# Operand buffers at multiples of 128 bytes, and score products ordered by their number of rows, in a two-block transformer kernel

## The chip, the cores and the metric

The kernel runs on one core of a Trainium2 chip. The metric is the device time of one launch in microseconds (us), the median of several runs. Engines: PE is TensorE (matrix products; PEld its weight loads), DVE is VectorE, ACT is ScalarE, POOL is GpSimd, SP is SyncE, whose queue here issues nearly all transfers.

## What is computed

256 tokens of width 1024 in float32 go through two transformer blocks of two layers each. The reference, cut to its frame:

```python
def first_block(x, p, ...):                       # 2 layers
    for i in range(2):
        z = rms_norm(h, g_mix[i]) @ w_in[i]
        y_a = chunked_spatial_gating(...)
        y_b = rwkv7_time_mix(...)
        y_c = nsa_attention(...)                  # compressed, selected and window branch; 8 query heads, 2 key groups
        h = h + concat([y_a, y_b, y_c]) @ w_out[i]
        hn = rms_norm(h, g_ffn[i])
        f = swiglu(hn, ...) if i % 2 == 0 else moe_swiglu(hn, router_w, router_b, w1, w3, w2)   # 8 experts, top 2
        h = h + f
        h = h + (p[i] @ ple_proj_w[i]) * sigmoid(rms_norm(h, g_ple[i]) @ ple_gate_w[i])

def second_block(x, ...):                         # 2 layers
    for l in range(2):
        x = x + 0.5 * swiglu(rms_norm(x), gate[l, 0], up[l, 0], down[l, 0])      # width 2816
        proj = rms_norm(x) @ w_in[l]
        ya, yb, yc = neighbourhood(...), diff_attention(...), window_gqa(...)
        g = sigmoid(h @ w_gate[l] + b_gate[l])
        x = x + sum(g_b * (y_b @ w_branch[l, b])) @ w_o[l]
        x = x + 0.5 * swiglu(rms_norm(x), gate[l, 1], up[l, 1], down[l, 1])

def moe_swiglu(x, router_w, router_b, w1, w3, w2):
    logits = x @ router_w + router_b
    top_v, top_i = lax.top_k(logits, 2)           # gate = softmax of the two
    for e in range(8):
        out = out + gate[..., e:e + 1] * swiglu(x, w1[e], w3[e], w2[e])
```

## The kernel before, in words

**The big products.** Weights and activations are split exactly into two float32r parts, high (`wh`) and low (`wl`), and each product is made of three passes (`mm`, L422, the matmul itself is L426): high by high, low by high, high by low. Most have 128 rows, a stationary operand of 128 x 128 (activations: `xT` of a normalised input, `xe` an expert's tokens, `gT` the gated middle of a feed-forward, `yT` an attention's output, `mT` the merged one) and move 512 columns of weights past it; in the profile's rows the moving operand stands first (`ps<-wh,xT`). The rest have the weights as the stationary operand and move 256 tokens (`ps<-xT,wh`).

**The weights.** `Feed` loads 1 MB pieces (`raw`, L193, on SP's queue) as far ahead as it has buffers, in the order of their use. ACT makes the high part (L215) and DVE the low part (L216) of each half. Each phase adds buffers of its own to the three of `wp`: a pool that is opened on top of what the pools below it take, so that a buffer's place depends on the sizes of all tiles ahead of it.

**The scores.** In the second block (`scores`, L1989, called 24 times) one call makes the scores of four heads for 128 queries: two heads `m` of each half `i` of the rows, in a bank for each half. Each is the sum of two products of 256 columns: one over all 128 rows (`ks`, L1996; it opens the sum, start=True) and one over the 64 rows of its half (`kl`, L1997, the remaining low part; it closes the sum, stop=True). They are written head by head, so 128 rows and 64 rows take turns. The first block's `first` in `nsa` (L1247) does the same (L1259, L1260), 16 products of 128 columns a call for the first tile of tokens and 8 of 256 columns for the second. Behind each call DVE takes the maximum (L1361), ACT the exponential (L1363), PE transposes the result (L1370), and products of the gates and branches, or of the RWKV chain, are woven in between.

**The router.** `experts` (L1436) makes the logits and picks two experts per token on DVE (L1485 to L1524); the index of each expert is taken from columns 256 to 263 of `const_moe` (`km["eidx"]`, used at L1493, L1497 and L1509), which is loaded at L1430, ahead of the first expert's weights. Then PE counts (L1515, L1516, L1527), DVE makes one-hot matrices `dp` (L1552), and PE gathers an expert's tokens with them (L1566). Products of the per-layer embedding (`pT`) fill in.

**What sets the order.** Each engine runs its instructions in the order of its queue. The Python code sets that order by generators whose steps are woven by fixed ratios, and a scheduler may move an instruction within it.

Of the kernel before, what the change touches and what calls it, by code (L numbers as in the profile page):

```python
# [22 lines left out]
P = 128  # L23
S = 256
# [11 lines left out]
# Big products run on operands that are split exactly into two float32r parts.  # L36
# [5 lines left out]
AHEAD = 4  # L42
FFN_BUFS = (4, 4)
# [5 lines left out]
# A mix's streams are merged by these numbers of steps: time before the units and its fill; time, units and their fill;  # L49
# the last steps of time and the first half of the output product.  # L50
# [14 lines left out]
def _t5_bucket(rel):  # L65
# [10 lines left out]
    ("gmmask", P), ("reset", 512), ("inv", 8),  # L76
]
_LAYOUTM = [("iota", 2 * P), ("eidx", 8)]
# [17 lines left out]
def _constants():  # L96
# [20 lines left out]
        "gmmask": s <= t, "reset": reset, "inv": np.broadcast_to(inv, (P, 8)),  # L117
# [3 lines left out]
        "eidx": np.broadcast_to(np.arange(8), (P, 8)),  # L121
# [10 lines left out]
    return {"const_ident": np.eye(P, dtype=np.float32), "const_first": c1, "const_moe": cm, "const_counts": np.concatenate([s < t, np.ones((P, P))], 1).astype(np.float32),  # L132
# [3 lines left out]
def _cols(w, at, n, step=512):  # L136
    """Column pieces of w from column at on."""
    return [w[:, c:c + min(step, at + n - c)] for c in range(at, at + n, step)]


def backwards(ap):
    """ap with its last dimension read from the end."""
# [6 lines left out]
class Feed:  # L149
    """The weights in the order of their use, loaded and split into float32r parts ahead of the products."""  # L150
# [12 lines left out]
    def drop(self, phase):  # L163
        """The buffers of a phase go."""
# [4 lines left out]
    def add(self, phase, srcs, split=True, heads=False):  # L169
        """srcs: DRAM [kb*128, n] in the order of their products; heads: columns (g j d) change to (j g d)."""  # L170
# [12 lines left out]
    def load(self):  # L183
        """Starts the next load, if a buffer is free."""
# [41 lines left out]
    def take(self, src):  # L226
        """The next row blocks of src: [(row block, part APs [128, n])]."""
# [6 lines left out]
    def done(self, n=1):  # L234
        """The products with the n oldest row blocks in hand are in the program."""
        for _ in range(n):
            self.free[1].append(self.live.popleft()[1])
# [11 lines left out]
class Operand:  # L249
    """Transposed parts [128, K, 256], put into the program by steps when products are about to need them."""  # L250
# [16 lines left out]
def merge(*streams):  # L267
    """The steps of all, each stream (steps, how many) kept as far along as the others."""
# [16 lines left out]
def weave(main, fill, ratio=1):  # L285
    """The steps of main with ratio steps of fill after each; what is left of fill stays."""
# [1942 lines left out]
```

## Time and profile before

| | |
|---|---|
| median of three runs | 2845.73 us (2842.85 to 2850.19) |
| span of the profiled execution | 2848.1 us; 2.4 us above the median; the page gives no other time for that execution |
| PE busy | 2794.6 us, 98% |
| DVE, ACT, POOL busy | 1911.7, 1652.1, 142.7 us |
| mean granted TensorE clock | 0.976 of full speed |
| moved by DMA | 594 MB, 209 GB/s over the span |

The span runs from the first to the last instruction. By stage: the first block's mixes, its dense feed-forward and embedding gates up to about 680 us, the experts up to about 1490 us, then the second block; its two attentions lie behind 1750 us and 2350 us. A matmul's record begins where the engine takes it up and its end is modelled; consecutive records overlap, so the pace is read from start to start, and the mean duration only shows differences between forms. Windows are given in us from the span's start.

### The profile page before, as it was taken

The page shows a single profiled execution, that of the slowest core. Times are in us where ns is not written, and L with a number is a line of the kernel's source. Part 1 is how long each engine was busy: PE and PEld are TensorE (multiplying, and loading weights), DVE is VectorE, ACT ScalarE, POOL GpSimd, SP SyncE. Part 2 cuts the span into 40 slices and gives each one's busy share as a digit, 9 for nine tenths or more (in the row PEclk, how much of TensorE's full clock was granted, in tenths as well). Part 3 has the DMA queues.
Part 4 walks back from the last instruction along what each step waited for, and adds up shares of the span by engine and source line. Part 5 has one row for each costly group of instructions (what it writes and reads, how often), then busy time and mean ns, then how long its engine had stood idle before and what let it go on. Part 6 is the DMA issues. An engine that isn't in the chain of part 4 may idle for free. (4 is left out here: it accounts for less than half of the span.)

```text
span 2848.1 us, 38806 instructions
## 1 busy us (share of the span) xinstructions
PE 2794.6 (98%) x15206; PEld 2308.7 (81%) x15206; DVE 1911.7 (67%) x2586; ACT 1652.1 (58%) x2277; POOL 142.7 (5%) x183
## 2 busy tenths in 40 slices
PE   8999999999999999999989999999999999999998
PEld 7888887877888888888877888888888888888887
DVE  6446556547989989988886556666555556676554
ACT  6445456436777777777766445664444445664543
POOL 1220001320000000000000000010000000010000
PEclk9889999979999999999999999999999999999999
DMA  6208533307999999999975745444654546444651
GB/s 210 88 21 280 185 127 124 105 16 282 344 338 360 337 347 353 342 348 336 348 247 197 240 156 151 140 137 168 236 185 177 186 137 180 134 141 152 245 191 60
DMA packets 301542, 594.46 MB, mean 209 GB/s; under 512 B 25926, under 2 KB 78886, under 8 KB 301350
## 3 DMA queue, kind: packets, MB, share of 16 engines
q1 hardware_dynamic: 300102, 587.69, 59.8%
q0 software_dynamic: 1248, 4.20, 0.5%
q8 instruction: 122, 2.00, 0.3%
q14 instruction: 70, 0.57, 0.1%
HBM read 590.74 MB, written 1.10 MB: 208 GB/s over the span
## 5 line engine op out<-in xcount | busy, mean ns | idle before, releaser
L216 DVE TENSOR_TENSOR wl<-raw,wh 128x1024 fp32r<-128x1024 f32 (+1 forms) x1098 | 1316.2, 1219 | 605.7 <-ACT wh L215 594.4
L215 ACT ACTIVATE wh<-raw 128x1024 fp32r<-128x1024 f32 x1098 | 1136.8, 1049 | 767.1 <-PE ps L426 715.7
L426 PE MATMUL ps<-wh,xT 128*128 128x512 f32 (+2 forms) x2944 | 919.3, 388 | 11.8 <-ACT xT L419 3.7
L426 PEld LDWEIGHTS ps<-wh,xT 128*128 128x128 f32 x2944 | 544.2, 190 | 133.6 <-DVE xT L420 7.6
L426 PE MATMUL ps<-wl,xT 128*128 128x512 f32 (+2 forms) x1472 | 563.1, 383 | 0.5 <-DVE wl L216 0.5
L426 PE MATMUL ps<-wh,gT 128*128 128x512 f32 x1584 | 504.4, 391 | 0.0
L426 PE MATMUL ps<-wh,xe 128*128 128x512 f32 (+1 forms) x1536 | 458.6, 378 | 0.0
L426 PEld LDWEIGHTS ps<-wh,gT 128*128 128x128 f32 x1584 | 297.2, 188 | 62.0
L426 PEld LDWEIGHTS ps<-wh,xe 128*128 128x128 f32 x1536 | 279.2, 188 | 55.7
L426 PEld LDWEIGHTS ps<-wl,xT 128*128 128x128 f32 x1472 | 279.7, 190 | 53.6 <-DVE wl L216 2.0
L426 PE MATMUL ps<-wl,gT 128*128 128x512 f32 x792 | 309.5, 391 | 0.0
L426 PE MATMUL ps<-wl,xe 128*128 128x512 f32 (+1 forms) x768 | 289.4, 377 | 1.4 <-DVE wl L216 1.2
L426 PE MATMUL ps<-xT,wh 128*128 128x256 f32 x960 | 178.1, 287 | 5.7 <-ACT wh L215 2.9
L426 PEld LDWEIGHTS ps<-wl,gT 128*128 128x128 f32 x792 | 148.8, 188 | 30.9 <-DVE wl L216 0.5
L426 PEld LDWEIGHTS ps<-wl,xe 128*128 128x128 f32 x768 | 144.3, 188 | 32.3 <-DVE wl L216 5.0
L426 PEld LDWEIGHTS ps<-xT,wh 128*128 128x128 f32 x960 | 150.4, 193 | 8.0 <-ACT wh L215 3.1
L426 PE MATMUL ps<-xT,wl 128*128 128x256 f32 x480 | 135.9, 284 | 0.0
L1363 ACT ACTIVATE e<-e,mx 128x256 f32<-128x256 f32 (+1 forms) x160 | 76.1, 477 | 43.9 <-DVE mx L1361 43.5
L426 PEld LDWEIGHTS ps<-xT,wl 128*128 128x128 f32 x480 | 92.2, 193 | 0.3 <-DVE wl L216 0.3
L493 ACT ACTIVATE junk<-x 128x512 bf16<-128x512 f32 x56 | 35.2, 628 | 62.4 <-DVE x L547 47.8
L417 DVE TENSOR_TENSOR gT<-ps,gT 128x512 fp32r<-128x512 f32 (+1 forms) x108 | 66.5, 639 | 6.0 <-ACT gT L416 6.0
L416 ACT ACTIVATE gT<-ps 128x512 fp32r<-128x512 f32 (+1 forms) x108 | 56.9, 551 | 19.2 <-PE ps L485 19.0
(434 smaller groups left out, 2470.2 us busy)
## 6 DMA issues: line engine op xcount, KB each, us to landing
raw<-in_moe_w_dram SPq DMA_DIRECT2D x264, 1024.0 KB, 6.2
raw<-in_w_in_dram SPq DMA_DIRECT2D x50, 1024.0 KB, 5.4
raw<-in_ffn_w_gate_dram SPq DMA_DIRECT2D x44, 1024.0 KB, 5.1
raw<-in_ffn_w_up_dram SPq DMA_DIRECT2D x44, 1024.0 KB, 5.0
raw<-in_ffn_w_down_dram SPq DMA_DIRECT2D x44, 1024.0 KB, 5.5
raw<-in_ffn_w_dram SPq DMA_DIRECT2D x33, 1024.0 KB, 5.1
raw<-in_w_gate_dram SPq DMA_DIRECT2D x24, 1024.0 KB, 5.0
raw<-in_w_branch_dram SPq DMA_DIRECT2D x12, 1024.0 KB, 4.9
```

The source lines that it names most:

```text
L215: nc.scalar.activation(ho, w, AF.Copy)
L216: nc.vector.tensor_tensor(lw, w, ho.bitcast(F32), op=ALU.subtract)
L416: nc.scalar.activation(h, src, AF.Copy)
L417: nc.vector.tensor_tensor(l, src, hf, op=ALU.subtract)
L426: self.nc.tensor.matmul(ps, lhs[p], rhs[q], start=start and i == 0, stop=stop and i == last)
L493: self.nc.scalar.activation(junk, self.x[:, t, h * 512:(h + 1) * 512], AF.Square, accum_out=ss[:, t, h:h + 1])
L1363: nc.scalar.activation(e[:, i], e[:, i], AF.Exp, bias=mx[:, i:i + 1], scale=-1.0, accum_out=sums[:, i:i + 1])
```

## The change

Two parts. **Places of the buffers:** tiles are padded, moved to another pool or share a buffer, so that the buffers of the big products' operands begin at multiples of 128 bytes. In the built programs their places, modulo 128, are:

| phase | weights, before | activations, before | both, after |
|---|---|---|---|
| mixes and dense feed-forward of the first block | 64 | xT 64, gT 64 | 0 |
| experts | 96 | xe 32, gT 96 | 0 |
| second block, first feed-forward | 32 (those of `wp` 64) | xT 64, gT 32 | 0 |
| second block, other three feed-forwards | 96 (`wp` 64) | xT 64, gT 96 | 0 |
| second block, attention and its products | 0 or 64 | xT 64, yT 96, mT 0 | 0 |

For this the expert indices leave `const_moe` and become a tile and a transfer of their own (`eidx`, 128 x 8, 4 KB), issued where the router's steps begin on DVE. **The scores:** `score_products` writes all products of 128 rows of a call first (only the first head of a bank opens it), then all of 64 rows, the halves taking turns (only the last closes it). Engines, shapes and number of products stay as they were; beside the one transfer nothing is added.

```diff
+PERS_REST = 12
-    ("gmmask", P), ("reset", 512), ("inv", 8),
+    ("gmmask", P), ("reset", 512), ("inv", 8), ("rest", 16),
-_LAYOUTM = [("iota", 2 * P), ("eidx", 8)]
+_LAYOUTM = [("iota", 2 * P)]
...
+        self.rb = self.pers.tile([P, NE], F32, name="rb")
...
-        r = self.xp.tile(shape, F32, name=self.nm("rs"), tag=f"rs{shape[1]}", bufs=3)
+        r = self.xp.tile(shape, F32, name=self.nm("rs"), tag=f"rs{shape[1]}", bufs=1 if shape[1] == 8 else 3)
...
-        self.oka = self.pers.tile([P, 4], F32, name="oka")
+        self.oka = self.pers.tile([P, PERS_REST], F32, name="oka")[:, 0:4]
...
-            for i in range(hb):
-                for gg, own, _ in self.halves():
-                    q = qs[t][:, j0 + i, gg]
-                    nc.tensor.matmul(pS[gg][:, i], q, ks[:, br, gg, 0:nk], start=True, stop=False)
-                    nc.tensor.matmul(pS[gg][:, i], q[own], kl[own, br, 0:nk], start=False, stop=True)
+            self.score_products([[(pS[gg][:, i], qs[t][:, j0 + i, gg], ks[:, br, gg, 0:nk], kl[:, br, 0:nk]) for gg in range(2)]
+                                 for i in range(hb)])
...
+        km["eidx"] = T("eidx", [P, NE])
+        nc.sync.dma_start(km["eidx"], a["const_eidx"])
         lg = T("lg", [P, NT, NE])
...
-            mx = T(f"mx{r}", [P, NT])
+            mx = pool.tile([P, NT], F32, name=f"mx{r}", tag=f"mx{r}")
...
-        cnt = T("cnt", [P, 1])
+        cnt = pool.tile([P, NT], F32, name="cnt", tag="mx0")[:, 0:1]
...
-        gs = pool.tile([P, 2], F32, name=self.nm("gs"), tag="gs", bufs=2)
+        gs = pool.tile([P, 16], F32, name=self.nm("gs"), tag="gs", bufs=2)[:, 0:2]
...
+    def score_products(self, heads):
+        last = len(heads) - 1
+        for m, two in enumerate(heads):
+            for ps, q, ks, _ in two:
+                self.nc.tensor.matmul(ps, q, ks, start=m == 0, stop=False)
+        for m, two in enumerate(heads):
+            for (_, own, _), (ps, q, _, kl) in zip(self.halves(), two):
+                self.nc.tensor.matmul(ps, q[own], kl[own], start=False, stop=m == last)
...
-            for m in range(2):
-                for i, own, _ in self.halves():
-                    q = qs[:, m, i, t * P:(t + 1) * P]
-                    nc.tensor.matmul(ps[i][:, m], q, ks[:, kb(m), i], start=True, stop=False)
-                    nc.tensor.matmul(ps[i][:, m], q[own], kl[own, kb(m)], start=False, stop=True)
+            self.score_products([[(ps[i][:, m], qs[:, m, i, t * P:(t + 1) * P], ks[:, kb(m), i], kl[:, kb(m)]) for i in range(2)]
+                                 for m in range(2)])
...
-                    ss = pool.tile([P, 4], F32, name=self.nm("oss"), tag="oss", bufs=2)
+                    ss = pool.tile([P, 4], F32, name=self.nm("oss"), tag="oss", bufs=1)
```

Left out: `tab`, `nsink` and `sink`, padded or moved in the same way, and comments. Lines move by up to three; the score products are L1916 (128 rows) and L1919 (64 rows) in the changed kernel, the big products L428.

**PE, the first score call of the second block** (`ks` are keys of 128 rows, `kl` of 64; `ps_19327` and `ps_19328` are the banks of the two halves). Before:

```order
8240 L426 MATMUL ps_19246<-xT_18858,wl_19175 128x256
8241 L1996 MATMUL ps_19327<-ks_19018,qs_19017 128x256
8242 L1997 MATMUL ps_19327<-kl_19019,qs_19017 128x256
8243 L1996 MATMUL ps_19328<-ks_19018,qs_19017 128x256
8244 L1997 MATMUL ps_19328<-kl_19019,qs_19017 128x256
8245 L1996 MATMUL ps_19327<-ks_19018,qs_19017 128x256
8246 L1997 MATMUL ps_19327<-kl_19019,qs_19017 128x256
8247 L1996 MATMUL ps_19328<-ks_19018,qs_19017 128x256
8248 L1997 MATMUL ps_19328<-kl_19019,qs_19017 128x256
8249 L426 MATMUL ps_19356<-wh_19205,xT_18858 128x512
```

In the changed kernel:

```order
8187 L428 MATMUL ps_19248<-xT_18860,wl_19177 128x256
8188 L1916 MATMUL ps_19329<-ks_19020,qs_19019 128x256
8189 L1916 MATMUL ps_19330<-ks_19020,qs_19019 128x256
8190 L1916 MATMUL ps_19329<-ks_19020,qs_19019 128x256
8191 L1916 MATMUL ps_19330<-ks_19020,qs_19019 128x256
8192 L1919 MATMUL ps_19329<-kl_19021,qs_19019 128x256
8193 L1919 MATMUL ps_19330<-kl_19021,qs_19019 128x256
8194 L1919 MATMUL ps_19329<-kl_19021,qs_19019 128x256
8195 L1919 MATMUL ps_19330<-kl_19021,qs_19019 128x256
8196 L428 MATMUL ps_19358<-wh_19207,xT_18860 128x512
```

Four goes to 64 rows become one. So stand 18 of the 24 calls; in the other six, and in most of the first block's calls, the scheduler puts other products in between or takes the banks one after the other, so that a call has two goes. Over the program there are 152 places before and 46 now where a product of 64 rows follows one of 128 in the score products.

**SP, the first loads of the experts.** Before:

```order
134 L193 DMA raw_5946<-in_moe_w_dram 128x2x1024
135 L193 DMA raw_6200<-in_moe_w_dram 128x2x1024
136 L193 DMA raw_6210<-in_moe_w_dram 128x4x512
137 L193 DMA raw_6233<-in_moe_w_dram 128x4x512
138 L193 DMA raw_6257<-in_moe_w_dram 128x4x512
```

In the changed kernel:

```order
135 L194 DMA raw_5946<-in_moe_w_dram 128x2x1024
136 L1469 DMA eidx<-in_const_eidx_dram 128x8
137 L194 DMA raw_6202<-in_moe_w_dram 128x2x1024
138 L194 DMA raw_6212<-in_moe_w_dram 128x4x512
139 L1543 TENSOR_LOAD cnti
140 L1543 ISA x2
141 L194 DMA raw_6235<-in_moe_w_dram 128x4x512
```

The indices are fetched behind the ninth load of expert weights (`raw_5946`). SP's read of the longest expert list (`cnti`), which stood at the end of the experts, now stands ahead of the twelfth.

**DVE, the router** (`lg` are the logits, `wl` the low part of expert weights). Before:

```order
677 L1490 TENSOR_REDUCE mx_6074<-lg 128x2
678 L1492 TENSOR_TENSOR ne_6076<-lg,mx_6074 128x16
679 L1493 SCALAR_TENSOR_TENSOR ne_6076<-ne_6076,const_moe 128x16
680 L1495 TENSOR_REDUCE first_6079<-ne_6076 128x2
681 L1497 TENSOR_TENSOR oh_6081<-const_moe,first_6079 128x16
```

In the changed kernel:

```order
674 L1491 TENSOR_REDUCE mx_6076<-lg 128x2
675 L1493 TENSOR_TENSOR ne_6078<-lg,mx_6076 128x16
676 L217 TENSOR_TENSOR wl_6205<-raw_5894,wh_6204 128x1024
677 L217 TENSOR_TENSOR wl_6209<-raw_5894,wh_6208 128x1024
678 L1494 SCALAR_TENSOR_TENSOR ne_6078<-ne_6078,eidx 128x16
679 L1510 TENSOR_SCALAR sel<-eidx 128x8
680 L1496 TENSOR_REDUCE first_6081<-ne_6078 128x2
681 L1498 TENSOR_TENSOR oh_6083<-eidx,first_6081 128x16
```

Two splits of weights now stand ahead of the first use of the indices. The second of them waits for PE to be done with the buffer of a late embedding product, and the instruction behind it waits for the transfer of `eidx`. On PE all embedding products now stand ahead of the counts.

## Rows read from the trace of the kernel before

**Rows 1.** The page's first part: busy time and share of the span.
```profile
PE 2794.6 (98%) x15206; PEld 2308.7 (81%) x15206; DVE 1911.7 (67%) x2586; ACT 1652.1 (58%) x2277; POOL 142.7 (5%) x183
```
**Rows 2.** Windows: length, PE, PEld, DVE, ACT, POOL busy, granted clock, DMA.
```profile
700.00:1450.00 750.00, 749.48 (x3626) 617.99 (x3626) 674.47 (x658) 575.85 (x618) 0.00 (x0) 1.00 0.96 346
...
558.20:571.90 13.70, 13.70 (x62) 10.24 (x62) 3.32 (x29) 6.49 (x26) 0.00 (x0) 0.50 0.01 1
...
1493.50:1496.90 3.40, 3.01 (x11) 2.69 (x12) 0.84 (x2) 2.10 (x8) 0.76 (x1) 0.50 0.31 98
```
**Rows 3.** Groups by form on PE, whole span: count, busy, mean ns, idle before.
```profile
L426 PE MATMUL ps<-wl,gT 128*128 128x512 f32 x792 | 309.5, 391 | 0.0
L426 PE MATMUL ps<-wl,xe 128*128 128x512 f32 x640 | 253.8, 397 | 0.9 <-DVE wl L216 0.7
```
**Rows 4.** The same view for 1755 to the end.
```profile
L426 PE MATMUL ps<-wl,xT 128*128 128x512 f32 x720 | 284.9, 396 | 0.0
```
**Rows 5.** Timeline of PE among the experts: start, duration, instruction.
```profile
701.42 0.39 PE L426 MATMUL ps<-wl,xe 128*128 128x512 f32 x1
...
708.42 0.39 PE L426 MATMUL ps<-wl,xe 128*128 128x512 f32 x1
...
710.05 0.62 PE L426 MATMUL ps<-wh,gT 128*128 128x512 f32 x2
...
713.46 0.62 PE L426 MATMUL ps<-wh,gT 128*128 128x512 f32 x2
```
**Rows 6.** Timeline of PE in the second block, a feed-forward's xT products.
```profile
2329.64 0.40 PE L426 MATMUL ps<-wl,xT 128*128 128x512 f32 x1
...
2333.16 0.39 PE L426 MATMUL ps<-wl,xT 128*128 128x512 f32 x1
```
**Rows 7.** Timeline of PE at the first score call of the second block.
```profile
1756.59 0.28 PE L426 MATMUL ps<-xT,wl 128*128 128x256 f32 x1
1756.70 0.28 PE L1996 MATMUL ps<-ks,qs 128*128 128x256 f32 x1
1756.91 0.38 PE L1997 MATMUL ps<-kl,qs 64*128 64x256 f32 x1
...
1759.10 0.50 PE L426 MATMUL ps<-wh,xT 128*128 128x512 f32 x1
```
**Rows 8.** Timeline of PE: products of 64 rows, both halves in turns, elsewhere.
```profile
47.23 0.48 PE L915 MATMUL ps<-tw,waup 64*128 64x256 f32 x1
47.24 0.48 PE L918 MATMUL ps<-zm,waup 64*128 64x256 f32 x1
47.55 0.38 PE L915 MATMUL ps<-tw,waup 64*128 64x256 f32 x1
```
**Rows 9.** Timeline of PE: a score call of 128 columns, first block.
```profile
555.22 0.33 PE L1259 MATMUL ps<-ks,qs 128*128 128x128 f32 x1
...
558.29 0.47 PE L1259 MATMUL ps<-ks,qs 128*128 128x128 f32 x1
```
**Rows 10.** Timeline of ACT and PE behind the second score call.
```profile
1766.25 0.19 ACT L1363 ACTIVATION_READ_ACCUMULATOR e<-e,mx 128x1 f32 x1
...
1767.26 0.93 PE L1370 MATMUL ps<-ident,e 128*128 128x128 f32 x7
```
**Rows 11.** Loads issued at 667.1 and 669.8: counts and starts, time to landing.
```profile
L193 SPq DMA_DIRECT2D raw<-in_moe_w_dram x2: 2582/2583/2584, 667.1 to 669.8; - x2
...
DMA to landing us min/median/max: 14.2/14.2/14.2
```
**Rows 12.** Timeline of DVE and PE: the router's first use of the indices, the first gather.
```profile
676.98 0.18 DVE L1493 SCALAR_TENSOR_TENSOR ne<-ne,const_moe 128x16 f32<-128x16 f32 x1
...
681.50 2.69 PE L1566 MATMUL ps<-dp,xT 128*128 128x128 f32 x20
```
**Rows 13.** Timeline of PE at the end of the experts, with the idle time before.
```profile
1493.89 1.94 PE L525 MATMUL ps<-ident,x 128*128 128x128 f32 x8 [5.45 <-PEq L1543]
```
**Rows 14.** The page's part 5: the low parts of the weights on DVE.
```profile
L216 DVE TENSOR_TENSOR wl<-raw,wh 128x1024 fp32r<-128x1024 f32 (+1 forms) x1098 | 1316.2, 1219 | 605.7 <-ACT wh L215 594.4
```

## Prediction before the run

> **What bounds the kernel now.** The page's first part comes first [rows 1]: PE is busy 98% of the span, DVE 67%, ACT 58%. A busy PE is not yet a PE at its peak, so the windows come next [rows 2]: among the experts PE is busy 749.48 of 750 us and DVE 674.47, which is 90%. The queue of products sets the time there, and time comes out of the span only if the products themselves follow each other faster. So I read PE's timeline from start to start and look for products that take longer than others of the same shape. There are two kinds. The reader should see [rows 5] that thirty products with `xe` start in 708.42 - 701.42 = 7.00 us, 233.3 ns each, and fifteen with `gT` in 713.46 - 710.05 = 3.41 us, 227.3 ns each: same shape, same clock, same engine without a gap. What differs is the place of the buffers (weights 96 and `xe` 32; weights 96 and `gT` 96). And a step between two products of 128 rows takes 0.11 us (1756.59 to 1756.70), the first step to 64 rows 0.21, and the seven steps from 1756.91 to 1759.10, in which rows change every time, 0.313 each [rows 7].
>
> **Places of the buffers.** Nothing is removed or added on PE; the pace of 512-column products is what can change. After the change all places are alike (0 and 0). I take the pace of the alike pair that I have, 227.3 ns.
> - Experts: 640 low-part products [rows 3], each with two high-part ones, so 1920 products; 1920 x (233.3 - 227.3) = 11.5 us. They lie in the stretch where PE has no gap, so this comes off the span if the weights keep up: DVE would then need 674.5 of 738.5 us, 91%.
> - `xT` in the second block from 1755 us on: 3 x 720 = 2160 products [rows 4]. In a plain stretch [rows 6] fifteen take 3.52 us, 234.7 ns each, 7.4 above `gT`; as a mean over all, which holds some pairs that are alike already, the duration is 396 ns against 391 of `gT` [rows 3, 4], 5 above. I take the mean: 2160 x 5 = 10.8 us. The upper end is 2160 x 7.4 = 16.0.
> - First block: places are alike already (64 and 64), so nothing. For the products that move 256 columns no row tells alike from unlike places; I take nothing.
>
> Sum -22 us, with ends -10 (only the experts gain) and -27. The Trainium skill speaks against this term: by the page SBUF — State Buffer, section Who interferes with whom, PE reads the moving operand and the weights through two independent ports that share nothing with each other, so the place of one against the other should not matter and the term would be 0. The rows do not agree with that, with 6 ns per product [rows 5]; but no run here has moved a buffer alone, so this stays as a rival.
>
> **The scores.** A call of the second block now takes 1759.10 - 1756.70 = 2.40 us [rows 7]. Grouped it is made of three steps between products of 128 rows, 3 x 0.11; one step to 64 rows, 0.21; the other half's product, which starts 0.01 later [rows 8]; the step to the second pair; again 0.01; and the step back to 128 rows, 0.31. The step to the second pair is not shown for this shape. It lies between 0.11 (no change of rows) and 0.32 (47.23 to 47.55, the same pattern with other operands [rows 8]); I take 0.22, the middle. Sum 1.09, saving 1.31. For 18 calls 23.6 us. In the six calls that stay in two goes a second pair of changes (0.21 + 0.31) comes back and one pair step goes; they save about 0.9 each, 5.4. Second block: 29 us.
>
> First block: eight calls of 256 columns, mostly in two goes, at 0.9 make 7. The four calls of 128 columns take 0.256 a step (555.22 to 558.29, twelve steps [rows 9]), 4.1 us; grouped, eight steps of at most 0.11, three pair steps of 0.22, changes of 0.52, and for three of them another 0.5: some 2.4. They save 1.7 each, 7. What hides these calls' end is the RWKV chain, in whose small products they are woven; shorter calls can leave PE waiting for it, so I take 11 of these 14. Together -40 us, ends -25 (nothing from the first block, 0.2 less from each call of the second) and -46.
>
> **The expert indices.** The new transfer is small, but it stands in SP's queue behind nine loads of 1 MB. The ninth is issued at 669.8 and lands 14.2 us later, at 684.0 [rows 11]. If transfers of a queue land in order, as these did, the indices are there at about 684.1. DVE wants them at 676.98 [rows 12], so it stands still 7.1 us with the router behind it. From there to the first gather on PE it is 681.50 - 676.98 = 4.52 us, less one split of 1.22 [rows 14] that now lies ahead: gather at 684.1 + 3.3 = 687.4, **5.9 us late**. Before, the embedding products covered the router; they are used up at about 681 whatever happens, so PE then idles. Behind an idle time of 5.45 us at the end of the experts [rows 13] the granted clock was 0.50 (1.2 GHz instead of 2.4) for 3.4 us [rows 2], half a stretch lost, 1.7. I take +7. Lower end +4: were the indices in time, the second split that was moved ahead would still wait for the last embedding products (681) and take 1.22, gather at 685.5. Upper end +12: the loads behind it (the twelfth waits for SP's read of the longest list, which comes from the same chain) arrive late once more. SP's read is then gone from the end of the experts; since the other engines read there as before, I take nothing for it.
>
> The padding, the smaller number of buffers for 1/rms (`rs`, `oss`) and the constant that is 1% longer touch engines with idle time [rows 1]: nothing, and with that cover gone some tenths of a us.
>
> **Sum.** -22 - 40 + 7 = -55 us. Against the profiled span of 2848.1 that is 2793; the span stands 2.4 above the median of the runs, so the forecast for the median is **2791 us**.
>
> **Rivals.**
> - *The softmax becomes the wait.* The last exponential ends at 1766.44 and its transposes begin at 1767.26 [rows 10]: 0.8 us of slack. A call 1.3 shorter brings the transposes 1.3 closer, while DVE may begin only when the bank is closed, now at the call's end rather than half-way, so the softmax moves by about 0.8: 0.3 of slack are left. If one split of weights (1.22) on DVE comes between, 0.9 is lost in each of 24 calls, 22 us: 2813. For it: the slack is small. Against it: splits have been there before, and the fill is long. Chance 0.13.
> - *The places bring nothing*, since something else slows the `xe` and `xT` products: -33, so 2813. Against it: the difference stands in both stretches [rows 5, 6] and goes with the places, not with the stage. Chance 0.10.
> - *The clock gains.* In the first block the clock was at half from 558.20 to 571.90 [rows 2], which begins inside a score call [rows 9]: what PE did before was twelve score products with rows changing. Denser products could keep it up: half of 13.7, 6.9 us, and the same once more in the other layer: 2777. Nothing in the profile shows that this call is the cause. Chance 0.08.
> - *Slower.* PE runs into the softmax in the second block and the clock falls behind each wait. Each of 24 calls then costs its wait w and, as above, 1.7: 24 x (w + 1.7) + 7 against 62 gained. From w = 0.6 on the kernel is slower; at w = 1.2, one split, it is +15, so 2860. For it: idle time did bring the clock down [rows 2, 13]. Against it: that was idle time of 5.45, and nothing here shows it after less than 1 us. Chance 0.04.
> - That the change does not arrive can be excluded for the order, which is in the program (46 changes to 64 rows instead of 152), and for the places.
>
> **How the numbers follow.** The forecast has 0.65. Its own ends are -10 - 25 + 12 = -23, 2823, and -27 - 46 + 4 = -69, 2777; the first two rivals lie inside, the third at the lower edge, and with the clock and the larger gains together it is 2766. The range is 2766 to 2824. About 0.3%, 8.5 us, is what a measurement of this kernel can tell from no change. All cases but the slower one are faster by more; that one reaches into the band at w near 0.6, and the eidx term could be larger than I think: faster 0.94, same 0.03, slower 0.03.
>
> **What would show it.** Right: `xe` and `xT` at 0.68 us per three products; score calls of 1.0 to 1.2 us; an idle time of PE of about 6 us ahead of the first gather, DVE waiting for `eidx`. Wrong: `xe` still at 0.70 (places); idle time ahead of L1370 (softmax); second pairs at 0.3 (pair step); the first gather less than 2 us after the last embedding product (indices); half-clock stretches that were not there before.

## The result and the profile after

The median is **2772.4 us** (2770.23 to 2782.28), against 2845.47 for the kernel before on the same chip: ratio 0.9747, 95% interval 0.9728 to 0.9766. The gain is 73 us where 55 were forecast. The profiled span is 2770.0 us, 78.1 below the one of before, and the mean granted clock 0.989 instead of 0.976. Executions of one kernel differ by how much of them runs at half the clock: the kernel before took 2828 to 2854 us on the chips used (clock 0.986 to 0.975), and one execution of the kernel with only the first tile's scores grouped, told below, took 4496 us at 0.553 and is left out of its figures.

The page's first part, as [rows 1]:

```profile
PE 2702.5 (98%) x15206; PEld 2265.9 (82%) x15206; DVE 1907.2 (69%) x2586; ACT 1650.8 (60%) x2277; POOL 141.9 (5%) x183
```

PE is busy for 92 us less with the same 15206 products, more than the span lost: some idle time is new. Where both lie is read by stage. The spans of the stages are taken from PE's timeline, from the first product of one to that of the next. The two columns on the right are experiments that do one half of the change each; they are told below. Times in us.

| stage | before | after | scores alone | places alone |
|---|---|---|---|---|
| first block, mixes of layer 0 | 228.4 | 204.4 | 207.1 | 218.5 |
| dense feed-forward, embedding gates | 190.4 | 190.5 | 190.5 | 190.5 |
| mixes of layer 1 | 241.4 | 210.4 | 209.0 | 239.8 |
| router, first expert | 69.9 | 79.9 | 70.3 | 79.6 |
| other experts | 755.7 | 748.4 | 755.5 | 748.4 |
| end of experts, first feed-forward of the second block | 231.3 | 225.9 | 228.9 | 226.2 |
| attention of layer 0 | 271.2 | 261.9 | 255.8 | 273.4 |
| two feed-forwards | 385.3 | 384.1 | 385.4 | 384.0 |
| attention of layer 1 | 272.3 | 263.0 | 258.1 | 275.4 |
| last feed-forward | 202.2 | 201.5 | 202.2 | 201.4 |

Three things stand out: the mixes gain 55.0 us, far more than any term of the sum gave them; the router loses 10; and the scores alone gain more in the attentions than the whole change does. Each is now read in the profile.

**The mixes: the clock.** Windows of both mixes and of the router, before (columns as [rows 2]):

```profile
0.00:228.40 228.40, 213.50 (x1708) 175.87 (x1709) 130.31 (x289) 115.42 (x220) 47.95 (x71) 0.87 0.36 117
418.80:660.20 241.40, 232.23 (x1791) 190.53 (x1790) 139.91 (x291) 117.06 (x229) 48.73 (x67) 0.88 0.27 87
660.20:730.10 69.90, 66.44 (x312) 50.95 (x310) 56.41 (x90) 48.10 (x60) 1.07 (x1) 0.98 0.94 345
```

The same stages after:

```profile
0.00:204.40 204.40, 188.56 (x1708) 158.38 (x1709) 129.77 (x289) 115.14 (x220) 47.92 (x71) 0.96 0.40 131
394.90:605.30 210.40, 201.08 (x1792) 168.08 (x1791) 137.82 (x291) 116.07 (x229) 47.85 (x67) 0.98 0.31 99
605.30:685.20 79.90, 70.55 (x312) 55.97 (x311) 56.09 (x90) 48.23 (x60) 1.07 (x1) 0.89 0.81 304
```

The number of products is the same, and the granted clock goes from 0.87 and 0.88 to 0.96 and 0.98. Narrower windows give the stretches at 0.50: before, four in each mix, 57.9 and 58.1 us long in all; after, two in each, 17.1 and 6.8. The sums over these eight and these four windows (length, then busy time):

```profile
sum 116.00, PE 112.53 PEld 92.15 DVE 46.26 ACT 35.06 POOL 20.76; mean PE 14.07 PEld 11.52 DVE 5.78 ACT 4.38 POOL 2.59
```

```profile
sum 23.90, PE 20.43 PEld 17.74 DVE 17.58 ACT 8.08 POOL 3.61; mean PE 5.11 PEld 4.43 DVE 4.39 ACT 2.02 POOL 0.90
```

If a stretch at 1.2 instead of 2.4 GHz costs half of itself, (116.0 - 23.9) / 2 = 46 of the 55 us are clock, and the remaining 9 are the shorter calls.

**The router: the indices and the splits.** PE and DVE at the counts, after (timeline as [rows 12]):

```profile
625.77 0.39 PE L428 MATMUL ps<-wh,pT 128*128 128x512 f32 x1
...
625.05 1.23 DVE L217 TENSOR_TENSOR wl<-raw,wh 128x1024 fp32r<-128x1024 f32 x1 [3.12 <-ACT wh L216]
627.77 1.23 DVE L217 TENSOR_TENSOR wl<-raw,wh 128x1024 fp32r<-128x1024 f32 x1 [1.49 <-ACT wh L216]
629.12 0.18 DVE L1494 SCALAR_TENSOR_TENSOR ne<-ne,eidx 128x16 f32<-128x16 f32 x1
...
631.22 0.38 PE L1516 MATMUL ps<-sel,counts 128*128 128x16 f32 x1 [5.06 <-DVE sel L1513]
```

The transfer itself, by its line (count, time of one, first and last issue, then the time to landing):

```profile
L1469 SPq DMA_DIRECT2D eidx<-in_const_eidx_dram x1: 1218/1218/1218, 618.1 to 618.1; - x1
...
DMA to landing us min/median/max: 10.9/10.9/10.9
```

4 KB take 10.9 us behind the loads of 1 MB, and land at 629.0. DVE does not stand idle for them: it waits 3.12 and 1.49 us for ACT's high parts of the two splits of weights that now stand ahead of the first use of the indices, and the second split ends at 627.77 + 1.23 = 629.0 too. Either would have held the router until then. PE, whose embedding products are used up, stands still for 5.06 us. What was not foreseen stands behind that idle time:

```profile
629.60:643.30 13.70, 11.56 (x48) 10.99 (x49) 5.18 (x27) 1.78 (x4) 0.00 (x0) 0.50 0.26 88
```

13.7 us at half the clock, four times the 3.4 of [rows 2]. By the two windows of the router above, PE's idle time grows from 69.90 - 66.44 = 3.5 to 79.90 - 70.55 = 9.4 us, and its busy time, for the same 312 products, from 66.4 to 70.6: 5.9 of the 10 us are waiting and 4.1 the clock.

**The scores of the second block.** The first call, as [rows 7]:

```profile
1704.06 0.63 PE L1916 MATMUL ps<-ks,qs 128*128 128x256 f32 x4
1704.62 0.50 PE L1919 MATMUL ps<-kl,qs 64*128 64x256 f32 x4
1705.05 0.50 PE L428 MATMUL ps<-wh,xT 128*128 128x512 f32 x1
```

From 1704.06 to 1705.05 a call takes 0.99 us instead of 2.40. Of the 18 calls in one piece twelve take 1.0 us, three take 1.3, and three are drawn out to 1.9 or 2.0 by a wait. In the second block PE nowhere waits ahead of the softmax's transposes (L1369), but one of those three calls, in layer 1, waits 0.8 us in its middle for DVE's maximum (L1360), which no call did before.

**Places, experts.** As [rows 5], the first and the last of 27 products of 512 columns:

```profile
657.71 0.39 PE L428 MATMUL ps<-wl,xe 128*128 128x512 f32 x1
...
663.83 0.39 PE L428 MATMUL ps<-wl,xe 128*128 128x512 f32 x1
```

6.12 us over 27 is 226.7 ns, against 233.3 before. The products of `xT` in the later feed-forwards did not follow: 36 of them take

```profile
2256.52 0.39 PE L428 MATMUL ps<-wl,xT 128*128 128x512 f32 x1
...
2264.88 0.39 PE L428 MATMUL ps<-wl,xT 128*128 128x512 f32 x1
```

8.36 us, 232.2 ns each, little less than the 234.7 of [rows 6]; the two feed-forwards gain 1.2 us.

**A new wait in the attentions.** Start of the attention of layer 0, after, on PE and DVE:

```profile
1669.06 0.56 DVE L1830 TENSOR_TENSOR na<-narows,colmask 128x384 f32<-128x384 f32 x1 [4.36 <-DMA narows<-rpbscr]
...
1672.73 1.01 PE L428 MATMUL ps<-wh,xT 128*128 128x512 f32 x2 [3.52 <-DVE xT L422]
```

With the scores alone:

```profile
1674.39 1.01 PE L426 MATMUL ps<-wh,xT 128*128 128x512 f32 x2 [0.69 <-DVE xT L420]
```

DVE's first addition of the position bias (`na`, L1830) waits 4.36 us for its rows to come back from memory. In the kernel before, six of the eight parts that DVE makes of `xT` stood ahead of it, now only four do: it has moved up by eleven instructions in DVE's order, and two more parts wait behind it. PE idles 3.52 us here and 3.6 in layer 1, with 3.4 us at half the clock behind each.

### The profile page after: what moved, and what is told of

Same layout as the page of the kernel before. It is cut to its first block, busy times and chain, and to the rows that moved or that the text cites. A ratio compares the mean times of both kernels' runs of the same rounds, so it can differ in the third digit from the quotient of the medians.

```text
span 2770.0 us, 38815 instructions
## 1 busy us (share of the span) xinstructions
PE 2702.5 (98%) x15206; PEld 2265.9 (82%) x15206; DVE 1907.2 (69%) x2586; ACT 1650.8 (60%) x2277; POOL 141.9 (5%) x183
## 5 line engine op out<-in xcount | busy, mean ns | idle before, releaser
L428 PE MATMUL ps<-wh,xT 128*128 128x512 f32 (+2 forms) x2944 | 915.5, 387 | 18.2 <-DVE xT L422 7.1
L428 PEld LDWEIGHTS ps<-wh,xT 128*128 128x128 f32 x2944 | 543.7, 190 | 135.4 <-DVE xT L422 10.9
L428 PE MATMUL ps<-wl,xT 128*128 128x512 f32 (+2 forms) x1472 | 561.8, 382 | 0.5 <-DVE wl L217 0.5
L428 PE MATMUL ps<-wh,gT 128*128 128x512 f32 x1584 | 504.2, 391 | 0.0
L428 PE MATMUL ps<-wh,xe 128*128 128x512 f32 (+1 forms) x1536 | 455.0, 375 | 0.0
L428 PEld LDWEIGHTS ps<-wh,gT 128*128 128x128 f32 x1584 | 297.2, 188 | 60.9
L428 PEld LDWEIGHTS ps<-wl,xT 128*128 128x128 f32 x1472 | 279.7, 190 | 52.4 <-DVE wl L217 2.1
L428 PEld LDWEIGHTS ps<-wh,xe 128*128 128x128 f32 x1536 | 280.9, 189 | 49.4
L428 PE MATMUL ps<-wl,gT 128*128 128x512 f32 x792 | 308.9, 390 | 0.0
L428 PE MATMUL ps<-wl,xe 128*128 128x512 f32 (+1 forms) x768 | 287.5, 374 | 1.6 <-DVE wl L217 1.4
L428 PE MATMUL ps<-xT,wh 128*128 128x256 f32 x960 | 178.9, 288 | 6.8 <-ACT wh L216 2.7
L428 PEld LDWEIGHTS ps<-wl,gT 128*128 128x128 f32 x792 | 148.8, 188 | 30.3 <-DVE wl L217 0.2
L428 PEld LDWEIGHTS ps<-wl,xe 128*128 128x128 f32 x768 | 145.1, 189 | 29.4 <-DVE wl L217 5.2
L428 PEld LDWEIGHTS ps<-xT,wh 128*128 128x128 f32 x960 | 150.8, 193 | 10.1 <-ACT wh L216 3.0
L428 PE MATMUL ps<-xT,wl 128*128 128x256 f32 x480 | 136.3, 285 | 0.0
L428 PEld LDWEIGHTS ps<-xT,wl 128*128 128x128 f32 x480 | 92.3, 193 | 0.3 <-DVE wl L217 0.3
L419 DVE TENSOR_TENSOR gT<-ps,gT 128x512 fp32r<-128x512 f32 (+1 forms) x108 | 66.4, 638 | 5.7 <-ACT gT L418 5.7
```

Source lines behind the costliest of these rows:

```text
L419: nc.vector.tensor_tensor(l, src, hf, op=ALU.subtract)
L428: self.nc.tensor.matmul(ps, lhs[p], rhs[q], start=start and i == 0, stop=stop and i == last)
```

## Experiments

The chips differ by a few us, so each ratio is to the kernel before on the same chip; kernels of one chip are compared directly.

### The two halves

**Places alone**: the changed kernel with the scores in turns again.

```diff
-        for m, two in enumerate(heads):
-            for ps, q, ks, _ in two:
-                self.nc.tensor.matmul(ps, q, ks, start=m == 0, stop=False)
-        ...
+        for m, two in enumerate(heads):
+            for (_, own, _), (ps, q, ks, kl) in zip(self.halves(), two):
+                self.nc.tensor.matmul(ps, q, ks, start=True, stop=False)
+                self.nc.tensor.matmul(ps, q[own], kl[own], start=False, stop=True)
```

> The changed kernel with the scores written head by head as before, 128 rows and 64 rows in turns; places and index transfer as changed. Theory A (the grouped scores hold the clock up in the first block's mixes, worth about 46 us of the 73): the half-clock stretches of the mixes come back, some 110 us up to the experts; what is left is 8 us won among the experts and some 4 in the second block against about 10 lost to the late indices, so 2840 to 2850 us. Theory B (the clock rose because buffers of the mixes have moved): the mixes keep the full clock, and the time is about 2800 us.

Measured: 2851.14 us, ratio 1.0004 (0.999 to 1.0018), as theory A said. The places' half as a whole brings nothing. The last column of the first table says why: -7.3 in the experts, -5.1 around the next feed-forward and -2.1 in the later ones are eaten by +9.7 at the router and +2.2 and +3.1 in the attentions. (2.4 of the 5.1 come without any move too, in the next column, by a stretch of the clock. And in the profiled execution, 2838.9 us, the second late stretch at half the clock of the first mix is missing although its calls take turns: its 218.5 us hold some 10 us of clock that are not the places'.)

**Scores alone**: the kernel before with `score_products` in both blocks, as in the change's diff.

> The kernel before with the scores grouped in both blocks; places as before, indices in the constant as before. Theory A: the mixes lose their half-clock stretches (46 us), the grouped calls give 9 us in the first block and about 16 in the second, so 2770 to 2780 us, as fast as the whole change. Theory B: the clock in the mixes stays as it was, and only the calls get shorter: about 2820 us.

Measured: 2765.78 us, ratio 0.9719 (0.9701 to 0.9737), below both forecasts, and not slower than the whole change (0.9747; the profiled spans are 2762.7 and 2770.0). All of the gain is in the scores. The calls of the second block were taken too low here, 16 us; the next run gives 29.

**Scores of the first block alone**: the same only in `nsa`.

> The kernel before with the scores grouped in the first block alone (12 calls). Theory A: about 55 us off, 46 of them by the clock, so 2787 to 2795 us, with less than 30 us at half clock up to the experts. Theory B: some 9 us off, 2836 us.

Measured: 2795.22 us, 0.9818 (0.9802 to 0.9834). Theory A holds again: the first block's calls are worth 53 us, the second block's 2795.22 - 2765.78 = 29.4.

### What in a score call costs

**The order of before, all products with 128 rows**: the second product of each pair moves all rows, and with them a product that the reference does not have.

```diff
-                    nc.tensor.matmul(pS[gg][:, i], q[own], kl[own, br, 0:nk], start=False, stop=True)
+                    nc.tensor.matmul(pS[gg][:, i], q, kl[:, br, 0:nk], start=False, stop=True)
...
-                    nc.tensor.matmul(ps[i][:, m], q[own], kl[own, kb(m)], start=False, stop=True)
+                    nc.tensor.matmul(ps[i][:, m], q, kl[:, kb(m)], start=False, stop=True)
```

> The kernel before, order of the score products as before (turns), but the second product of each pair takes all 128 rows instead of the 64 of its half, so that the number of rows never changes; it adds the other half's product to the sum, which the reference does not have. If it is the change of rows that costs: a call of the second block takes 8 x 0.12 = 0.95 us instead of 2.40, the half-clock stretches of the mixes go, and the time is that of e2 or some us less, 2760 to 2768 us. If it is the order of opening and closing a sum (each sum closed before the next is opened): the calls stay at 2.4 us and the time at 2845.

Measured: 2761.08 us, 0.9712 (0.9679 to 0.9746), granted clock 0.995. The first call:

```profile
1699.76 0.28 PE L1996 MATMUL ps<-ks,qs 128*128 128x256 f32 x1
1699.88 0.28 PE L1997 MATMUL ps<-kl,qs 128*128 128x256 f32 x1
...
1700.72 0.40 PE L426 MATMUL ps<-wh,xT 128*128 128x512 f32 x1
```

Eight steps of 0.12, a call of 0.96 us, although sums are still opened and closed in turns, and the mixes take 207.4 and 210.7 us, as with the grouped scores. It is the change of rows that costs, in the calls and by the clock, not the order of opening and closing.

### Which calls bring the clock down

Grouped only for the **first tile** of tokens (`t == 0`, products of 128 columns), then only for the **second** (`t == 1`, 256 columns):

```diff
-            for i in range(hb):
-                ...
+            if t == 0:
+                self.score_products(...)
+            else:
+                for i in range(hb):
+                    ...
```

> The kernel before with the scores grouped only in the first block's calls for the first tile of tokens (four calls of 16 products of 128 columns). Theory P (each half-clock stretch of a mix belongs to the calls just ahead of it): the stretches at 131.6 and 558.2 go, those at 182.8 and 588.9 stay; 14 us by the clock and 5 by the calls, about 2829 us. Theory Q (one kind of call decides for the whole mix): nothing but the 5 us, about 2843, or nearly all of the 52 of e3, about 2795.

> The kernel before with the scores grouped only in the first block's calls for the second tile of tokens (eight calls of 8 products of 256 columns). Theory P: the stretches at 182.8 and 588.9 go, those at 131.6 and 558.2 stay; 29 us by the clock and 5 by the calls, about 2814 us. Theory Q: about 2843 or about 2795, the other way round from e7.

Measured: 2807 to 2815 us, 0.9886 (0.9846 to 0.9926), and 2809 to 2814 us, 0.9886 (0.9854 to 0.9917): 32 us for either alone, which together would be 65 where both at once give 52 (0.9818). Theory P holds for the second tile's 2814; for the first tile it said 2829, and Q fits neither. Windows around the four late stretches (two in each layer), before:

```profile
100.00:150.00 50.00, 49.71 (x521) 39.10 (x518) 24.41 (x73) 25.45 (x64) 8.06 (x15) 0.86 0.29 97
150.00:205.00 55.00, 54.94 (x454) 44.66 (x452) 26.07 (x70) 25.92 (x58) 14.91 (x11) 0.81 0.06 20
530.00:565.00 35.00, 35.00 (x414) 27.23 (x412) 17.13 (x48) 16.02 (x37) 8.13 (x15) 0.90 0.18 62
565.00:630.00 65.00, 64.22 (x402) 51.02 (x402) 26.41 (x83) 26.03 (x71) 13.74 (x10) 0.66 0.05 17
```

First tile grouped:

```profile
100.00:150.00 50.00, 49.26 (x549) 39.15 (x548) 29.25 (x82) 29.00 (x72) 10.70 (x18) 1.00 0.28 94
150.00:205.00 55.00, 54.94 (x468) 45.26 (x468) 27.62 (x81) 25.16 (x53) 13.30 (x10) 0.81 0.06 21
530.00:565.00 35.00, 34.35 (x351) 27.19 (x345) 20.89 (x73) 22.14 (x56) 7.29 (x9) 1.00 0.19 62
565.00:622.00 57.00, 56.00 (x506) 44.97 (x505) 36.98 (x98) 25.74 (x64) 11.09 (x9) 1.00 0.15 45
```

Second tile grouped:

```profile
100.00:150.00 50.00, 49.80 (x532) 39.35 (x531) 25.20 (x73) 24.61 (x63) 8.06 (x15) 0.86 0.30 104
150.00:205.00 55.00, 54.47 (x533) 45.41 (x531) 34.81 (x96) 31.00 (x65) 17.00 (x13) 1.00 0.12 39
530.00:565.00 35.00, 34.91 (x268) 25.97 (x267) 15.44 (x60) 16.88 (x49) 1.67 (x3) 0.80 0.15 46
565.00:622.00 57.00, 55.10 (x522) 45.65 (x521) 38.09 (x101) 26.93 (x63) 17.04 (x13) 1.00 0.09 30
```

In layer 0 each tile's stretch goes with its own calls and the other stays: 0.86 turns to 1.00 with the first tile alone, 0.81 with the second alone. In layer 1 the first stretch goes with the first tile's calls, while the second (0.66) goes with either group; that is where theory P failed for the first tile. So calls whose rows keep changing are what brings the clock down here, but not each by itself. Which call answers for which stretch rests on one profile of each kernel, and with the places alone the second stretch of layer 0 was missing without any grouping. How the chip decides stays open.

### The places

**The indices early**: the transfer of `eidx` is issued 51 us into the program, into unused columns of another tile; the places stay.

```diff
-        self.oka = self.pers.tile([P, PERS_REST], F32, name="oka")[:, 0:4]
+        rest = self.pers.tile([P, PERS_REST], F32, name="oka")
+        self.oka, self.eidx = rest[:, 0:4], rest[:, 4:4 + NE]
...
+            nc.sync.dma_start(self.eidx, a["const_eidx"])
...
-        km["eidx"] = T("eidx", [P, NE])
-        nc.sync.dma_start(km["eidx"], a["const_eidx"])
+        T("eidx", [P, NE])
```

> The changed kernel with the 4 KB of expert indices read into eight spare columns of another small tile in the beginning of the program. If the indices' place behind nine loads costs what the trace says (idle time of PE of 6 us ahead of the first gather and a half-clock stretch behind it), the time falls by 8 to 11 us to 2761 to 2764 us, with no idle time of PE over 2 us ahead of the gather. If the router was late for another reason (the embedding products that now stand ahead of the counts), it stays within 3 us of 2772.

Measured: 2760.28 us, 0.969 (0.9674 to 0.9706), on the chip of the two halves: 5.5 below the scores alone. The router's window is back:

```profile
608.10:676.80 68.70, 65.51 (x311) 50.92 (x310) 56.04 (x89) 48.13 (x60) 1.07 (x1) 0.98 0.94 345
```

68.7 us at clock 0.98, against 69.9 before and 79.9 in the change: the router's whole loss is gone, its half-clock stretch included. That the late landing alone made this loss is not shown, for the order of DVE went back with it; the split now stands behind the router's steps:

```profile
627.45 0.18 DVE L1521 COPY pos<-ps 128x16 f32<-128x16 f32 x1
627.54 1.22 DVE L217 TENSOR_TENSOR wl<-raw,wh 128x1024 fp32r<-128x1024 f32 x1
```

The run with the places alone speaks for the order. There the transfer is issued at 660.9 and lands 11.0 us later, at 671.9; DVE is still busy with the second split, goes on without a wait for the indices, and PE stands still for 4.94 us all the same:

```profile
670.77 1.23 DVE L217 TENSOR_TENSOR wl<-raw,wh 128x1024 fp32r<-128x1024 f32 x1 [1.49 <-ACT wh L216]
672.00 0.17 DVE L1494 SCALAR_TENSOR_TENSOR ne<-ne,eidx 128x16 f32<-128x16 f32 x1
```

An early transfer with the splits still ahead was not run.

**`xe` moved by 32 bytes**, on top of that. With it move the tiles that stand beside it in its pool, the experts' outputs `ye` and the small `lgT`; the weights, `gT` and all others keep their places.

```diff
+            shift = pool.tile([P, NE], F32, name="shift")
...
-        T("eidx", [P, NE])
```

> As e4, with one buffer moved alone: the experts' tokens xe by 32 bytes, from 128 to 160 modulo 256, weights left at 128. If the place of the activations against the weights sets the pace, 1920 products go from 227.5 back to 233 ns: 10 to 11 us above e4, 2770 to 2772. If something else made the experts faster in the changed kernel, as e4, 2758 to 2762.

Measured: 2773.38 us, 0.9752 (0.9721 to 0.9783). 21 products take

```profile
651.68 0.40 PE L428 MATMUL ps<-wl,xe 128*128 128x512 f32 x1
...
656.58 0.40 PE L428 MATMUL ps<-wl,xe 128*128 128x512 f32 x1
```

4.90 us, 233.3 ns each: the pace of before is back with this move, and an expert takes 100.4 us instead of 99.1, from gather to gather. By the Trainium skill, SBUF — State Buffer, section Who interferes with whom, PE reads the moving operand and the weights through independent ports. If that meant that the place of one against the other cannot matter, this run disagrees, by 6.6 ns per product, in products of which only `xe` was moved.

**Weights and `xT` alike modulo 256**: in the changed kernel the later feed-forwards' weights stand 128 bytes off a multiple of 256 and `xT` on one. A tile of 128 bytes moves weights and `gT` together.

```diff
+                        if l or f:
+                            shift = fp.tile([P, 32], F32, name=f"shift{l}{f}")
```

> The changed kernel with the early indices (as in e4) and the buffers of the three later feed-forwards of the second block moved by 128 bytes, so that weights and xT are alike modulo 256 and not only modulo 128. Theory M256 (what counts is the place modulo 256; in the changed kernel weights at 128 and xT at 0 still run at 232.5 ns): their xT products fall to 227.5, some 1440 to 1600 products by 5 ns, 7 to 8 us below e4, 2752 to 2754 us. Theory M128 (alike modulo 128 is enough, xT is slower for another reason): as e4, 2758 to 2762.

Measured: 2754.17 us, 0.9689 (0.9665 to 0.9714), and once more on another chip:

> e6 once more, on the same chip as e10, so that the two can be compared: 2752 to 2756 us.

2757.19 us, 0.9705 (0.9681 to 0.973). The 48 products between these rows now take 10.88 us, 226.7 ns each:

```profile
2240.11 0.39 PE L428 MATMUL ps<-wl,xT 128*128 128x512 f32 x1
...
2250.99 0.39 PE L428 MATMUL ps<-wl,xT 128*128 128x512 f32 x1
```

The three feed-forwards fall by 2.5, 2.4 and 2.7 us (192.5 to 190.0, 191.5 to 189.1, 201.6 to 198.9). The ratios are too wide to show these 7.6 us (0.969 without the edit); the profiled spans (2758.6 and 2752.5), the stages and the pace do. What counts for the products of 512 columns in these runs is that both places are alike modulo 256: 226.7 ns where they are, 232.2 at 128 bytes apart, 233.3 at 32. In the attentions, too, the weight buffers of that phase stand 128 bytes off `xT`; they were not moved.

### The bias addition

In the kernel with early indices and places alike modulo 256, the first `na` addition is made to depend on the last part of `xT`, and the products at the attention's start are no longer woven with the bias steps.

```diff
+                if h == 0:
+                    one = self.eidx[:, 0:1]
+                    nc.vector.tensor_scalar(one, w["after"](), 0.0, 1.0, op0=ALU.mult, op1=ALU.add)
+                    nc.vector.scalar_tensor_tensor(w["na"][:, h], backwards(rows), one, ..., op0=ALU.mult, op1=ALU.add)
...
-        weave(start, sw["steps"], 2)
+        run(islice(sw["steps"], 1))
+        run(start)
+        sw["after"] = lambda: xT.parts[1].bitcast(F32)[:, KD - 1, S - 1:S]
...
-        weave(chain(*made1), sw["steps"], 2)
+        weave(chain(*made1), sw["steps"], 4)
```

> As e6, with the first table of position biases of each attention in the second block made on DVE only after the attention's operand xT is split (it takes a factor 1 that is made from the last part of xT). In the changed kernel DVE holds that addition ahead of two splits of xT while its rows are still on the way from DRAM, PE waits 3.5 us in each layer, and a half-clock stretch of 3.4 us lies behind it. If that is a cost of the order alone: 2 x (2 to 3 us less idle time + 1.7 us by the clock), 6 to 10 us below e6, 2744 to 2748. If PE would have waited for its operand anyway: within 2 us of e6.

Measured: **2741.65 us**, 0.9648 (0.9625 to 0.9671), 15.5 below the kernel without this edit on the same chip, and the fastest of all. DVE makes `xT` first:

```profile
1661.32 0.48 DVE L422 SCALAR_TENSOR_TENSOR xT<-ps,col,xT 128x256 fp32r<-128x256 f32 x1 [0.55 <-ACT xT L421]
...
1662.03 0.62 DVE L1835 SCALAR_TENSOR_TENSOR na<-narows,oka,colmask 128x384 f32<-128x384 f32 x1
```

The attentions go from 259.2 and 262.0 to 255.4 and 255.5, which is 10.3 us, by the order of DVE and the weaving together. The other 5 lie in stretches of the clock in stages that the edit does not touch; whether it moved them or they fell so by chance stays open.

## Why the prediction was right in size and wrong in its terms

The forecast of 2791 is within 0.7% and the range held the time, but partly by luck, with errors of opposite sign. Where the sum had -55, the stages give about -79 (the span -78): -48 of clock that it put at nothing (46 in the mixes, 2.4 behind the experts), -38 of shorter calls (-40 forecast), -13 of places (-22), +10 at the router (+7) and +11 in the attentions, which stood in no term.

1. **The clock (0.08 as a rival, 6.9 us twice): wrong.** The step that failed is "Nothing in the profile shows that this call is the cause", for which the sum took nothing. The prediction priced one stretch at 0.50 and its like. The stretches of both mixes were there to be read, 116 us of them, and 92 went. The grouping gave back 46 us by the clock, more than any other term: the first block's calls alone are worth 53, and their own shortening was put at 14 at most.
2. **The scores of the second block (29 us): right**, 29.4 between the two runs; the first call takes 0.99 us where 1.09 was worked out. The step to the second pair is 0.22, as taken; the step back to 128 rows is 0.21, where 0.31 was taken from calls in which the rows change at every step.
3. **The scores of the first block (11 us): right as far as it can be told**, 55.0 - 46 = 9 once the clock is taken out.
4. **The places (-22 us): mechanism right, size wrong, three times.** In the experts 11.5 were forecast; the seven of the stage gave 7.3, which makes 8.3 for eight. The pace of the 512-column products fell as forecast in plain stretches, and from 233.4 to 227.9 ns as a mean over the stage. The step that failed is "For the products that move 256 columns no row tells alike from unlike places; I take nothing". They go the other way:

Before and after, the group by form, columns as [rows 3]:

```profile
L426 PE MATMUL ps<-wh,xe 128*128 128x256 f32 x256 | 45.8, 279 | 0.0
```

```profile
L428 PE MATMUL ps<-wh,xe 128*128 128x256 f32 x256 | 47.9, 285 | 0.0
```

From start to start they went from 114 to 119.7 ns; 384 such products give back 2.2 us. For `xT` (10.8) the failed step is "After the change all places are alike (0 and 0)": alike modulo 128 they are, but the pace goes by 256, and the later feed-forwards kept one operand 128 bytes off. They gained 1.9 us in all. And the sum began at 1755 us: the first feed-forward of the second block, unlike before and alike after, was left out and gained 3.0 against the scores alone.

5. **The indices (+7 us): size near, mechanism half right.** The transfer landed when forecast, 684.0 in the time of the kernel before, and the first gather came 6.2 us later in its stage than before, where 5.9 were forecast. But "it stands still 7.1 us" for the indices is not what DVE did: the splits ahead of them kept it until the same moment. The lower end, with the splits alone (the gather at 685.5), failed; it let the second split begin once PE had left the buffer, and left out that ACT makes the high part first. That both ended together is luck. Behind PE's wait the stretch at half the clock was taken as 3.4 us, by a row from another place, and was 13.7, so that the clock took 4.1 instead of 1.7. The stage lost 10.0.
6. **Not foreseen: the bias addition.** DVE's first addition of the attentions moved up, ahead of two more parts of `xT`. The order of DVE there stood in no term of the sum. Against the scores alone the attentions lose 6.1 and 4.9 us. Why the scheduler moved it was not tried; just ahead of its rows the transfer of `sink` has left SP's queue.
7. **The rivals.** The softmax became the wait in one call, for 0.8 us. That the places bring nothing is wrong as a mechanism (moving `xe` costs the pace) and right as a sum (ratio 1.0004): what they bring in the big products they lose at the router and in the attentions. The slower case did not come.

## What to carry to other kernels

Read the granted clock stage by stage before summing anything: an engine that is busy 98% of the time can stand at half its clock for a whole stretch, and what one edit does to such stretches can outweigh its direct effect. Keep small products of different row counts apart, or give them all the same rows, even if that means more arithmetic (the run that did so also added a product that does not belong in the sum; with zeros in those rows the result would be that of the reference, which was not run). When tiles move for the sake of their places, compare the order of every queue afterwards, since two splits ahead of the router's steps, or one addition in front of a wait, cost as much here as the places brought.

## What the runs showed of the hardware

- Products of 512 columns follow each other in 226.7 to 227.3 ns where the weights' and the activations' places are alike modulo 256 and in 232.2 to 234.7 ns where they are not (233.3 at 32 and at 64 bytes apart, 232.2 at 128); the products of 256 columns with `xe` go the other way, 114 ns at 64 bytes apart, 118.3 at 32 and 119.7 alike.
- Between products of 256 columns, a step with a change between 128 and 64 rows takes 0.21 us where the change stands alone and 0.313 where rows change at every step, against 0.12 without a change, although the smaller product does less.
- The granted clock can be at half while PE has no gap: 13.70 of 13.70 us busy at 0.50 [rows 2]. With the rows of the score products all alike, such stretches went.
- Two idle times of PE of nearly the same length were followed by very different stretches at half the clock: 5.45 us by 3.4 [rows 2, 13], 5.06 us by 13.7. What sets the length was not tried.
